# The second half of an MLP: 24 pairs of K tiles in sliding groups, all by seven products, their sums gathered in DRAM

## The chip, the cores and the metric

The kernel runs on one core of one Trainium2 chip. The metric is the device time of one execution in microseconds (us), as the median of several runs. TensorE is PE in the views of the profile, VectorE is DVE, ScalarE is ACT, GpSimd is POOL and SyncE is SP.

## The reference

One layer of a decoder on 512 rows of width 2048: a mixer of gated linear attention and mLSTM heads, a layer norm, an MLP with squared ReLU, and a second layer norm. The change lies in the second matrix product of the MLP.

```
def _sq_relu_mlp(u, w_ff1, w_ff2):
    return jnp.square(jax.nn.relu(u @ w_ff1)) @ w_ff2
...
    u = x * (1.0 + sc2) + sh2
    y = _sq_relu_mlp(u, w_ff1[l], w_ff2[l])
    x = _layer_norm(ALPHA * x + g2 * y, ln2_g[l], ln2_b[l])
```

`w_ff1` is 2048 x 8192 and `w_ff2` 8192 x 2048. The hidden matrix h (512 x 8192) is the left operand of the second product.

## The kernel before

**Split operands.** Every float32 operand of a matmul is split into a high and a low part: ACT casts the high part, DVE subtracts it to get the low part, and PE multiplies high by high, high by low and low by high into the same bank of PSUM. So each product costs three matmuls.

**First half of the MLP.** w_ff1 is worked through in 16 blocks of 512 columns, each over 8 steps (units) of two K tiles. From the third block on, a unit is a Strassen-like 2 x 2 scheme with seven products in place of eight: each product is 6 matmuls of 256 columns, and it has a PSUM bank of its own. `w_operands` prepares the weight side of such a unit: a cast of three quarters as they are (`bh`), four sums of quarters on DVE (`w_combos`), a cast of the sums (`th`, in the views `hi`), and two subtractions (`bl`, 768 wide, and `tl`, in the views `lo`, 1024 wide). A unit is prepared two units ahead (`LOOK`), and its tiles have three buffers. At the end of a block the seven banks are combined by two copies on ACT and seven additions on DVE; ReLU, square and a store of h to the DRAM tiles `hd` follow.

**Second half.** h comes back from `hd` in pairs of K tiles. 30 pairs go through 4 column blocks of 512; the last two pairs (`tail`) are added while the layer norm runs. The 30 pairs are cut into chunks of 8, 8, 8 and 6. For each chunk the four column blocks follow one another, and one pass over a chunk for one block (a sweep) keeps its sums in PSUM. A pair is of kind S (seven products, 42 matmuls of 256 columns) or C (eight products as plain matmuls, 24 of 512 columns). The four chunks have 4, 5, 4 and 0 pairs of kind S, over four blocks 52 S units and 44 + 24 C units.

`load` prepares the h side of a pair (`h_operands`): for S an own set of casts on ACT and of sums and subtractions on DVE, once for the four sweeps that use it; for C two casts and two subtractions. Loads of the next chunk are spread over the last sweep of the chunk before. At the end of a sweep one ACT copy and DVE additions empty the banks into `z` in SBUF (`evac1` to `evac3`).

**What sets the order.** DVE and ACT run their instructions exactly as the code issues them (`MANUAL`): in each pass of the unit loop first the operands of unit n + 2, then the jobs of unit n (loads among them), then the matmuls of unit n, then, after the last unit of a sweep, its emptying. PE, SP and POOL follow an order that the framework chooses. PSUM has eight banks, handed out in turn by `mm_bank`.

Of the kernel before, what the change touches and what calls it, by code (L numbers as in the profile page):

```python
# [16 lines left out]
P = 128  # L17
# [41 lines left out]
def trunk_layer_kernel(  # L59
# [989 lines left out]

    pa21 = tc.alloc_tile_pool(name="pa21", bufs=1, side="right")  # L1050
# [72 lines left out]
    def sums_add(i):  # L1123
# [30 lines left out]
    def w_combos(raw, name, f_slot):  # L1154
        b12, b11, b22, b21 = (raw[:, j * HB:(j + 1) * HB] for j in range(4))
        f = f_slot(name + "f")
        t3, n1, t2, t4 = (f[:, j * HB:(j + 1) * HB] for j in range(4))
        V.tensor_tensor(n1, b11, b12, ALU.subtract)  # L1158
        V.tensor_tensor(t3, b22, b12, ALU.subtract)  # L1159
        V.tensor_tensor(t2, b22, n1, ALU.add)  # L1160
        V.tensor_tensor(t4, b21, t2, ALU.subtract)  # L1161
        return f

# [6 lines left out]
    def w_ops(bh, bl, th, tl):  # L1170
        def op(h, l, j):
# [3 lines left out]
                7: op(th, tl, 0), 5: op(th, tl, 1), 6: op(th, tl, 2), 4: op(th, tl, 3)}  # L1175
# [49 lines left out]
    def assign(kinds):  # L1225
        free, out, odd = {"h": 16, "l": 16, "s": NS}, [], False
        for kind in kinds:
            want = ("hhhhlll", "hhhllll")[odd] if kind == "S" else "hhll"
            odd ^= kind == "S"
            if want.count("h") > free["h"] or want.count("l") > free["l"]:  # L1230
                n = len(want)
                want = ("s" * min(n, free["s"]) + "h" * free["h"] + "l" * free["l"])[:n]
            for g in want:
                free[g] -= 1
            assert min(free.values()) >= 0
            out.append(want)
        return out
# [109 lines left out]
    for nb in range(2, DFF // CB):  # L1347
        pb = {m: mm_bank(f"fp{nb}_{m}", (P, 2, HB)) for m in ORDER}
        for i in range(KP):
# [10 lines left out]
            if nb == DFF // CB - 1 and i in EARLY:  # L1360
                load(0, EARLY.index(i))
# [302 lines left out]
```

## Time and profile before

| | us |
|---|---|
| median of 3 runs | 2192.06 (2190.67 to 2193.08) |
| the profiled execution, its own time | 2191.13 |
| its span | 2189.1 |
| PE busy | 2134.7 (98%) |
| DVE busy | 1689.8 (77%) |
| ACT busy | 861.5 (39%) |
| POOL busy | 125.9 (6%) |

The span is the time from the first to the last recorded instruction; some 2 us of the execution's own time lie around it. Busy time is summed over records, and neighbouring records of one engine can overlap by some tens of nanoseconds, so the spacing of starts tells what an instruction costs in a row. The granted TensorE clock is 1.00 of its full level in every stretch shown below. In the part of the page on DMA queues there is no queue that POOL's software feeds: every transfer of data is issued from SP.

### The profile page before, as it was taken

Reading aid. Unit: us, or ns where it says so; the run is one execution under the profiler, and the core shown is the slowest. Engines: PE = TensorE matmul, PEld = TensorE weight load, DVE = VectorE, ACT = ScalarE, POOL = GpSimd, SP = SyncE. Lnnn points to the kernel's source line nnn. Section 1 sums busy time; section 2 is a strip of 40 time slices with the busy share of each in tenths; the row PEclk is TensorE's granted clock in tenths of the full one; section 3 lists DMA queues with packets and bytes.
Section 4 is the critical chain, followed back from the end, with each engine's and each line's share of the span. In section 5 each row is a group of like instructions: output and inputs, shape, how many; then the busy total and the mean of one; then the engine's idle time right before and its main releaser. Section 6 shows DMA issues by size and latency. Waiting matters only on the chain.

```text
span 2189.1 us, 33107 instructions
## 1 busy us (share of the span) xinstructions
PE 2134.7 (98%) x13105; PEld 1909.0 (87%) x13105; DVE 1689.8 (77%) x2848; ACT 861.5 (39%) x1184; POOL 125.9 (6%) x107
## 2 busy tenths in 40 slices
PE   6989999999999999999999999999999999999997
PEld 4767788888888888999999999999999999998886
DVE  7986677667776878888788788788768779666678
ACT  4222544243332135454454454455334334323223
POOL 3334200100000000000000000000000000000002
PEclk9999999999999999999999999999999999999999
DMA  8875345666678766444444444355334335335562
GB/s 312 273 271 177 119 136 154 215 217 226 216 236 303 273 207 225 141 130 151 128 132 136 126 136 135 116 163 174 106 106 154 119 105 164 125 103 186 169 199 85
DMA packets 174407, 374.81 MB, mean 171 GB/s; under 512 B 16032, under 2 KB 18300, under 8 KB 174252
## 3 DMA queue, kind: packets, MB, share of 16 engines
q1 hardware_dynamic: 174252, 372.70, 52.3%
q8 instruction: 102, 1.67, 0.3%
q14 instruction: 53, 0.43, 0.1%
HBM read 347.40 MB, written 25.18 MB: 170 GB/s over the span
## 4 chain that ended last, share of the span: by engine, by line
PE 82%; DVE 7%; DMA 6%; ACT 2%; issue 2%; POOL 0%; SPq 0%; DVEq 0%; ACTq 0%; POOLq 0%
PE fp L1357 9%; PE fp L1358 9%; PE fp L1356 9%; PE gp_c L1450 3%; PE gp_c L1451 3%; PE gp_c L1452 3%; DMA wr<-in_w_ada_dram 3%; DVE wr L162 2%; PE gp L1436 2%; PE gp L1438 2%; PE gp L1439 2%; PE gp L1545 2%; PE gp L1547 2%; PE gp L1546 2%; PE gp_c L1439 2%
## 5 line engine op out<-in xcount | busy, mean ns | idle before, releaser
L162 DVE SCALAR_TENSOR_TENSOR wr<-wr,csb 128x1024 f32<-128x1024 f32 x192 | 256.9, 1358 | 28.5 <-DMA wr<-in_w_ada_dram 28.2
L1598 POOL TENSOR_TENSOR l2lrs<-l2lrs,neghalf 128x1 f32<-128x1 f32 x3 | 1.6, 543 | 1307.7 <-DVE l2lrs L1597 1307.7
L1161 DVE TENSOR_TENSOR z<-f,z 128x256 f32<-128x256 f32 x125 | 53.1, 425 | 4.3
L1158 DVE TENSOR_TENSOR z<-f 128x256 f32<-128x256 f32 x125 | 52.4, 419 | 0.0
L1159 DVE TENSOR_TENSOR z<-f 128x256 f32<-128x256 f32 x125 | 52.4, 419 | 0.0
L1160 DVE TENSOR_TENSOR z<-f,z 128x256 f32<-128x256 f32 x125 | 52.4, 419 | 0.0
L1382 ACT ACTIVATE z<-z 128x1024 f32<-128x1024 f32 x28 | 28.1, 1052 | 54.7 <-DVE z L1377 54.7
L1189 DVE TENSOR_TENSOR f_0lo<-z,f_0hi 128x1024 fp32r<-128x1024 f32 x17 | 20.8, 1226 | 22.3 <-ACT f_0hi L1185 22.3
L1185 ACT CAST f_4hi<-z 128x1024 fp32r<-128x1024 f32 x17 | 17.9, 1053 | 43.5 <-DVE z L1161 43.5
L1185 ACT CAST f_0hi<-z 128x1024 fp32r<-128x1024 f32 x17 | 17.8, 1049 | 38.3 <-PE fp L1357 24.5
L1189 DVE TENSOR_TENSOR f_1lo<-z,f_1hi 128x1024 fp32r<-128x1024 f32 x14 | 17.2, 1226 | 18.5 <-ACT f_1hi L1185 18.5
L654 DVE TENSOR_TENSOR gqk<-gqk,st 128x512 f32<-128x512 f32 x40 | 25.3, 679 | 7.5 <-PE st L223 7.3
L654 DVE TENSOR_TENSOR gv<-gv,st 128x512 f32<-128x512 f32 x40 | 25.2, 679 | 5.9 <-PE st L230 5.8
L1189 DVE TENSOR_TENSOR f_7lo<-z,f_7hi 128x1024 fp32r<-128x1024 f32 x14 | 17.2, 1226 | 15.1 <-ACT f_7hi L1185 15.1
L126 DVE TENSOR_TENSOR ul<-uf,uh 128x512 fp32r<-128x512 f32 x16 | 11.9, 752 | 21.0 <-ACT uh L125 21.0
L1386 ACT ACTIVATE z<-z 128x1024 f32<-128x1024 f32 x28 | 28.0, 1048 | 0.0
L832 ACT ACTIVATE y<-mo,dd 128x256 f32<-128x256 f32 x16 | 7.6, 475 | 51.9 <-DVE dd L825 51.9
L1185 ACT CAST f_6hi<-z 128x1024 fp32r<-128x1024 f32 x14 | 14.7, 1053 | 29.6 <-DVE z L1161 29.6
L1185 ACT CAST f_1hi<-z 128x1024 fp32r<-128x1024 f32 x14 | 14.7, 1049 | 29.5 <-PE fp L1357 26.5
L1185 ACT CAST f_5hi<-z 128x1024 fp32r<-128x1024 f32 x14 | 14.7, 1051 | 28.9 <-DVE z L1161 28.9
L1185 ACT CAST f_7hi<-z 128x1024 fp32r<-128x1024 f32 x14 | 14.7, 1049 | 28.7 <-PE fp L1357 24.5
L1373 DVE TENSOR_TENSOR z<-z,fp 128x512 f32<-128x512 f32 x14 | 9.6, 688 | 20.7 <-PE fp L1358 20.7
(2266 smaller groups left out, 8781.9 us busy)
## 6 DMA issues: line engine op xcount, KB each, us to landing
f<-in_w_ff_dram SPq DMA_DIRECT2D x232, 512.0 KB, 3.8
wr<-in_w_ada_dram SPq DMA_DIRECT2D x192, 512.0 KB, 4.7
hd<-z SPq DMA_DIRECT2D x32, 512.0 KB, 3.9
hr<-hd SPq DMA_DIRECT2D x26, 512.0 KB, 3.5
z<-in_x_dram SPq DMA_DIRECT2D x4, 1024.0 KB, 5.4
xd<-z SPq DMA_DIRECT2D x4, 1024.0 KB, 8.5
x<-xd SPq DMA_DIRECT2D x16, 256.0 KB, 4.4
wl<-in_w_ff_dram SPq DMA_DIRECT2D x8, 512.0 KB, 4.7
```

The source lines that it names most:

```text
L162: V.scalar_tensor_tensor(raw, raw, 1.0, csb[:, h * DH:(h + 1) * DH], ALU.mult, ALU.mult, accum_out=msum[:, h, v * KT + k:v * KT + k + 1])
L1158: V.tensor_tensor(n1, b11, b12, ALU.subtract)
L1161: V.tensor_tensor(t4, b21, t2, ALU.subtract)
L1185: A.copy(th, f)
L1189: V.tensor_tensor(tl, f, th, ALU.subtract)
L1356: T.matmul(o, lhsT=wh[:, sl], rhs=q[:, 0], start=i == 0 and j == 0, stop=False)
L1357: T.matmul(o, lhsT=wh[:, sl], rhs=q[:, 1], start=False, stop=False)
L1358: T.matmul(o, lhsT=wl[:, sl], rhs=q[:, 0], start=False, stop=i == KP - 1 and j == 1)
L1439: T.matmul(o, lhsT=ql[:, sl], rhs=wh, start=False, stop=last and own and j == 1)
L1450: T.matmul(o[:, cl], lhsT=qh[:, sl], rhs=hi[:, t, cl], start=False, stop=False)
L1451: T.matmul(o, lhsT=qh[:, sl], rhs=lo[:, t], start=False, stop=False)
L1452: T.matmul(o, lhsT=ql[:, sl], rhs=hi[:, t], start=False, stop=last and t == 1)
```

## The change

All 24 pairs of the first three chunks become kind S (96 units); the six pairs of the last chunk stay C. The chunks give way to groups of two pairs. A round takes up to four neighbouring groups (8 units) through one column block, and the next round drops the oldest group, takes in a new one and goes on to the next block, so that each pair is used in four rounds in a row. There are 15 rounds of 2, 4, 6, 8 (nine times), 6, 4 and 2 units. Two pairs are loaded per full round, for the even pair at its first unit, for the odd one at its fifth.

Every round holds its seven sums in seven banks and ends with `evac`: ACT copies the banks two by two into a scratch of 128 x 1024 in `z` (three such pieces in turn), and each filled piece goes to the DRAM tile `sums` of its block. The first round of a block stores it from SP; the eleven later ones add it with an accumulating transfer, issued from POOL. In the plain sweeps at the end `sums_load` brings the sums back (28 transfers of 256 KB), and `z_sums` combines them on DVE (7 additions for each block). The signs of the scheme are turned so that two sums of 256 columns with a common term become one instruction of 512, in the weights of both halves and in h. The seven PSUM additions that empty a block of the first half stay seven.

```diff
@@ -1154,12 +1160,15 @@
     def w_combos(raw, name, f_slot):
         b12, b11, b22, b21 = (raw[:, j * HB:(j + 1) * HB] for j in range(4))
         f = f_slot(name + "f")
-        t3, n1, t2, t4 = (f[:, j * HB:(j + 1) * HB] for j in range(4))
-        V.tensor_tensor(n1, b11, b12, ALU.subtract)
-        V.tensor_tensor(t3, b22, b12, ALU.subtract)
+        n1, t3, t2, t4 = (f[:, j * HB:(j + 1) * HB] for j in range(4))
+        V.tensor_tensor(halves(f[:, :S]), halves(raw[:, HB:3 * HB]),
+                        b12.unsqueeze(1).to_broadcast([P, 2, HB]), ALU.add)
         V.tensor_tensor(t2, b22, n1, ALU.add)
-        V.tensor_tensor(t4, b21, t2, ALU.subtract)
+        V.tensor_tensor(t4, b21, t2, ALU.add)
...
-    NS = 17
-    CHUNKS = ["SCSCSCSC", "SCSSCSSC", "SCSCSCSC", "CCCCCC"]
-    SLOTS = [assign(kinds) for kinds in CHUNKS]
+    NS, SP, GP, CP = 28, 24, 2, 6
+    S_SLOTS = ("hhhhlll", "hhhllll", "hhhhlll", "hhhllll", "hhllsss") + ("sssssss",) * 3
...
-        a1 = slot(tags[2], f"hb{ft}")
-        split(a1[:, :HB], a1[:, HB:], raw[:, 0, :HB])
-        f = f_slot(f"hf{ft}")
-        s1, s2, s3, s4 = (f[:, j * HB:(j + 1) * HB] for j in range(4))
-        a11, a21, a12, a22 = (raw[:, t, o:o + HB] for t in range(2) for o in (0, HB))
-        V.tensor_tensor(s1, a21, a22, ALU.add)
+        a2h, a2l, a1, c1h, c1l, c2h, c2l = (slot(g, f"h{ft}_{i}") for i, g in enumerate(tags))
+        a11, a21, a12, _ = (raw[:, t, o:o + HB] for t in range(2) for o in (0, HB))
+        f = f1_slot(f"hf{ft}")
+        s3, s1, s2, s4 = (f[:, j * HB:(j + 1) * HB] for j in range(4))
+        A.copy(a2h, raw[:, 1])
+        A.copy(a1[:, :HB], a11)
+        V.tensor_tensor(halves(f[:, :S]), a21.unsqueeze(1).to_broadcast([P, 2, HB]),
+                        raw.rearrange("p t (o c) -> p (t o) c", o=2)[:, 0:4:3], ALU.subtract)
         V.tensor_tensor(s2, s1, a11, ALU.subtract)
-        V.tensor_tensor(s3, a11, a21, ALU.subtract)
-        V.tensor_tensor(s4, a12, s2, ALU.subtract)
-        s12 = h_split(f[:, :S], tags[3:5], f"hc{ft}")
-        s34 = h_split(f[:, S:], tags[5:7], f"hd{ft}")
+        V.tensor_tensor(s4, a12, s2, ALU.add)
+        A.copy(c1h, f[:, :S])
+        A.copy(c2h, f[:, S:])
+        V.tensor_tensor(a2l, raw[:, 1], a2h, ALU.subtract)
+        V.tensor_tensor(a1[:, HB:], a11, a1[:, :HB], ALU.subtract)
+        V.tensor_tensor(c1l, f[:, :S], c1h, ALU.subtract)
+        V.tensor_tensor(c2l, f[:, S:], c2h, ALU.subtract)
...
+    NG = SP // GP
+    units = []
+    for r in range(NG + 3):
+        ps = [GP * g + e for g in range(max(0, r - 3), min(NG - 1, r) + 1) for e in range(GP)]
+        units += [("S", (r + 1) % NCB, 2 * p, p == ps[0], p == ps[-1]) for p in ps]
+    NU = len(units)
+    for b in range(NCB):
+        units += [("C", b, 2 * (SP + i), i == 0, i == CP - 1) for i in range(CP)]
+    tail = 2 * (SP + CP)
...
+    for p in range(GP, SP + CP):
+        use = [u[2] for u in units].index(2 * p)
+        n = max(1, use - 6 + 3 * (p % 2)) if p < SP else NU - 10 + 2 * (p - SP)
+        at(n, lambda p=p: load(p))
+        if p >= 2 * GP:
+            at(n - 2, lambda p=p: fetch(2 * p, p % 2))
...
+    sums = [hdram.tile([P, 7 * S], F32, name=f"sums{b}") for b in range(NCB)]
+    begun = set()
+    def evac(pb, b):
+        for i in range(0, 7, 2):
+            ms = ORDER[i:i + 2]
+            st_ = scratch("st", 2, 3)[:, :len(ms) * S]
+            for e, m in enumerate(ms):
+                A.copy(halves(st_[:, e * S:(e + 1) * S]), pb[m])
+            o = sums[b][:, i * S:(i + len(ms)) * S]
+            if b in begun:
+                G.dma_start(o, st_, accum_op=ALU.add)
+            else:
+                nc.sync.dma_start(o, st_)
+        begun.add(b)
+    def sums_load(b, q):
+        for i, m in enumerate(ORDER):
+            q[m] = f3_slot(f"q{b}_{m}")
+            nc.sync.dma_start(q[m], sums[b][:, i * S:(i + 1) * S])
...
+        if last and kind == "S":
+            evac(pb, b)
```

Where ACT stands at the border of the two halves: after the last copy out of the first half's last block (`fp`) come, before, loads of pairs (`ha` to `hd`) and the operands of units 2 and 3 (`f_0_4`, `f_0_6`).

```order
L1371 COPY z<-fp_3_14003 128x2x256
L125 CAST ha_14510<-z 128x512
L125 CAST hb_14514<-z 128x256
L125 CAST hc_14521<-z 128x512
L125 CAST hd_14525<-z 128x512
L1181 CAST f_0_4bh<-f_0_4_14529 128x768
L1185 CAST f_0_4hi<-z 128x1024
L125 CAST ha_14585<-z 128x512
L125 CAST hb_14589<-z 128x512
L1382 ACTIVATE z<-z 128x1024 x2
L125 CAST f_0_6hi<-f_0_6_14595 128x1024
L125 CAST ha_14627<-z 128x512
```

Now the operands of units 2 and 3 (`f_2_0`, `f_2_2`), the ReLU and square of the last block and the load of pair 2 (`h_0` to `h_5`) stand in front of the first copy of the first round's banks (`gp_1`).

```order
L1376 COPY z<-fp_3_13897 128x2x256
L1190 CAST f_2_0bh<-f_2_0_14414 128x768
L1387 ACTIVATE z<-z 128x1024 x2
L1194 CAST f_2_0hi<-z 128x1024
L1391 ACTIVATE z<-z 128x1024 x2
L1273 CAST h_0_14475<-z 128x512
L1274 CAST h_2_14477<-z 128x256
L1279 CAST h_3_14478<-z 128x512
L1280 CAST h_5_14480<-z 128x512
L1190 CAST f_2_2bh<-f_2_2_14493 128x768
L1194 CAST f_2_2hi<-z 128x1024
L1457 COPY z<-gp_1_14407 128x512
```

The seven copies that empty the first round stand behind the operands of unit 3, though that round ends with unit 1.

Where ACT empties a full sweep, before (second chunk, block 1): one copy between the operands of the next block.

```order
L1185 CAST f_2_16hi<-f_2_16f 128x1024
L1465 COPY fq_1_0_16950<-gp_1_1_16591 128x2x256
L125 CAST f_2_18hi<-f_2_18_16957 128x1024
L1181 CAST f_2_20bh<-f_2_20_16999 128x768
L1185 CAST f_2_20hi<-f_2_20f 128x1024
L1181 CAST f_2_22bh<-f_2_22_17057 128x768
```

Now, after the fourth round (block 0; the next units are `f_1_4` to `f_1_8`):

```order
L1190 CAST f_1_6bh<-f_1_6_15632 128x768
L1194 CAST f_1_6hi<-z 128x1024
L1457 COPY z<-gp_1_15202 128x512
L1457 COPY z<-gp_2_15203 128x512
L1457 COPY z<-gp_3_15204 128x512
L1457 COPY z<-gp_7_15205 128x512
L1457 COPY z<-gp_5_15206 128x512
L1457 COPY z<-gp_6_15207 128x512
L1457 COPY z<-gp_4_15208 128x512
L1190 CAST f_1_8bh<-f_1_8_15705 128x768
L1194 CAST f_1_8hi<-z 128x1024
L1273 CAST h_0_15718<-z 128x512
```

Seven copies follow one another; the operands of the next round's third unit (`f_1_8`) and the load of a pair (`h_0`) stand behind them.

Where DVE prepares the weights of one S unit, before (`f_1_20`, block 1, K tiles 20 and 21):

```order
L1158 TENSOR_TENSOR f_1_20f<-f_1_20_16599 128x256
L1159 TENSOR_TENSOR f_1_20f<-f_1_20_16599 128x256
L1160 TENSOR_TENSOR f_1_20f<-f_1_20_16599,f_1_20f 128x256
L1161 TENSOR_TENSOR f_1_20f<-f_1_20_16599,f_1_20f 128x256
L1188 TENSOR_TENSOR f_1_20bl<-f_1_20_16599,f_1_20bh 128x768
L1189 TENSOR_TENSOR f_1_20lo<-f_1_20f,f_1_20hi 128x1024
```

And now:

```order
L1164 TENSOR_TENSOR z<-f_1_20_17560 128x512
L1166 TENSOR_TENSOR z<-f_1_20_17560,z 128x256
L1167 TENSOR_TENSOR z<-f_1_20_17560,z 128x256
L1197 TENSOR_TENSOR f_1_20bl<-f_1_20_17560,f_1_20bh 128x768
L1198 TENSOR_TENSOR f_1_20lo<-z,f_1_20hi 128x1024
```

Two sums have become one of twice the width, and each of the two sums left reads the result of the instruction ahead of it.

## Rows read from the trace of the kernel before

**Rows 1.** Busy time in three stretches of the second half: engines, clock, DMA.

```profile
core 0: us, PE busy (x) PEld busy (x) DVE busy (x) ACT busy (x) POOL busy (x), PEclk, DMA share, GB/s
1500.00:1540.00 40.00, 39.59 (x255) 35.83 (x254) 35.41 (x63) 23.10 (x33) 0.00 (x0) 1.00 0.45 148
1820.00:1860.00 40.00, 40.00 (x275) 37.20 (x274) 38.45 (x67) 19.03 (x29) 0.00 (x0) 1.00 0.53 170
2060.00:2100.00 40.00, 40.00 (x179) 33.12 (x178) 27.75 (x38) 9.71 (x11) 0.00 (x0) 1.00 0.55 165
```

**Rows 2.** Waits of PE from 1510 us to the end.

```profile
PE gp_c L1439 <- DVE hd L126: 0.2, 1, 0.2
PE gp L1436 <- ACT f_8hi L1185: 0.2, 1, 0.2
```

**Rows 3.** Timeline of PE: start us, us, engine, line, operation.

```profile
1499.87 0.28 PE L1436 MATMUL gp<-f_0bh,hb 128*128 128x256 f32 x1
...
1679.16 0.28 PE L1436 MATMUL gp<-f_20bh,hb 128*128 128x256 f32 x1
...
1684.17 0.28 PE L1436 MATMUL gp<-f_22bh,hb 128*128 128x256 f32 x1
...
2002.07 0.39 PE L1545 MATMUL gp<-f_48hi,hb 128*128 128x512 f32 x1
```

**Rows 4.** Timeline of DVE in the last columns of the first half.

```profile
1474.60 0.68 DVE L126 TENSOR_TENSOR ha<-hr,ha 128x512 fp32r<-128x512 f32 x1
...
1477.78 0.69 DVE L126 TENSOR_TENSOR hd<-z,hd 128x512 fp32r<-128x512 f32 x1
1478.38 0.42 DVE L1158 TENSOR_TENSOR z<-f 128x256 f32<-128x256 f32 x1
...
1479.05 0.42 DVE L1160 TENSOR_TENSOR z<-f,z 128x256 f32<-128x256 f32 x1
1479.51 0.42 DVE L1161 TENSOR_TENSOR z<-f,z 128x256 f32<-128x256 f32 x1
1479.85 0.95 DVE L1188 TENSOR_TENSOR f_5bl<-f,f_5bh 128x768 fp32r<-128x768 f32 x1
1481.13 1.22 DVE L1189 TENSOR_TENSOR f_5lo<-z,f_5hi 128x1024 fp32r<-128x1024 f32 x1 [0.32 <-ACT f_5hi L1185]
1482.27 0.69 DVE L126 TENSOR_TENSOR ha<-hr,ha 128x512 fp32r<-128x512 f32 x1
```

**Rows 5.** Timeline of DVE where a column block of the first half is emptied.

```profile
1459.14 0.69 DVE L1373 TENSOR_TENSOR z<-z,fp 128x512 f32<-128x512 f32 x1 [1.48 <-PE fp L1358]
1459.86 0.69 DVE L1374 TENSOR_TENSOR z<-z,fp 128x512 f32<-128x512 f32 x1
...
1462.98 0.42 DVE L1158 TENSOR_TENSOR z<-f 128x256 f32<-128x256 f32 x1
```

**Rows 6.** Timeline of ACT: casts, and a copy out of PSUM.

```profile
1477.65 0.83 ACT L1181 CAST f_5bh<-f 128x768 fp32r<-128x768 f32 x1
1480.04 1.05 ACT L1185 CAST f_5hi<-z 128x1024 fp32r<-128x1024 f32 x1 [1.56 <-DVE z L1161]
...
1538.16 1.06 ACT L1185 CAST f_0hi<-z 128x1024 fp32r<-128x1024 f32 x1 [2.26 <-DVE z L1161]
1539.12 0.58 ACT L1465 COPY fq<-gp 128x512 f32<-128x512 f32 x1
1539.59 1.06 ACT L125 CAST f_2hi<-f 128x1024 fp32r<-128x1024 f32 x1
```

**Rows 7.** DMA issues: out<-in, queue, count, KB each, median us to landing.

```profile
hd<-z SPq DMA_DIRECT2D x32, 512.0 KB, 3.9
hr<-hd SPq DMA_DIRECT2D x26, 512.0 KB, 3.5
...
xd<-z SPq DMA_DIRECT2D x4, 1024.0 KB, 8.5
...
out_dram<-z SPq DMA_DIRECT2D x16, 256.0 KB, 2.3
```

More of the change, by code (lines that the diff above doesn't have):

```diff
@@ L1432, in seven @@
             (wh, wl), (qh, ql) = ops[m], hq[m]
[L1433 removed]
             for j in range(2):
[L1435 to L1437 removed]
+                o, sl = pb[m][:, j], slice(j * P, (j + 1) * P)
+                T.matmul(o, lhsT=qh[:, sl], rhs=wh, start=first and j == 0, stop=False)
                 T.matmul(o, lhsT=qh[:, sl], rhs=wl, start=False, stop=False)
[L1439 removed]
+                T.matmul(o, lhsT=ql[:, sl], rhs=wh, start=False, stop=last and j == 1)
@@ L1441, in plain @@
     def plain(pb, ops, hq, first, last):
         hi, lo = ops
-        for t in range(2):
-            qh, ql = hq[t]
-            for tt in range(NT):
-                o, sl = pb["C"][tt], slice(tt * P, (tt + 1) * P)
-                for cl in ((slice(0, HB), slice(HB, CB)) if first and t == 0 and tt > 1
-                           else (slice(0, CB),)):
-                    T.matmul(o[:, cl], lhsT=qh[:, sl], rhs=hi[:, t, cl], start=False, stop=False)
-                T.matmul(o, lhsT=qh[:, sl], rhs=lo[:, t], start=False, stop=False)
-                T.matmul(o, lhsT=ql[:, sl], rhs=hi[:, t], start=False, stop=last and t == 1)
@@ new lines, in plain @@
+        for tt in range(NT):
+            sl = slice(tt * P, (tt + 1) * P)
+            for t in range(2):
+                uh, ul = hq[t]
+                T.matmul(pb[tt], lhsT=uh[:, sl], rhs=hi[:, t], start=first and t == 0, stop=False)
+                T.matmul(pb[tt], lhsT=uh[:, sl], rhs=lo[:, t], start=False, stop=False)
+                T.matmul(pb[tt], lhsT=ul[:, sl], rhs=hi[:, t], start=False, stop=last and t == 1)
+    sums = [hdram.tile([P, 7 * S], F32, name=f"sums{b}") for b in range(NCB)]
@@ new lines, in z_sums @@
+    def z_sums(b, q):
+        c11, c12, c21, c22 = (z[:, b, 2 * i:2 * i + 2, o:o + HB] for i in range(2) for o in (HB, 0))
+        p = {m: halves(t) for m, t in q.items()}
+        V.tensor_tensor(c11, p[1], p[2], ALU.add)
+        V.tensor_tensor(p[6], p[1], p[6], ALU.add)
+        V.tensor_tensor(p[7], p[6], p[7], ALU.subtract)
+        V.tensor_tensor(p[6], p[6], p[5], ALU.subtract)
+        yield
+        V.tensor_tensor(c12, p[3], p[6], ALU.subtract)
+        V.tensor_tensor(c21, p[7], p[4], ALU.add)
+        V.tensor_tensor(c22, p[5], p[7], ALU.subtract)
+        yield
@@ new lines, in trunk_layer_kernel @@
+    g2b = []
+    for n, (kind, b, ft, first, last) in enumerate(units):
+        if first and kind == "S":
+            pb = {m: mm_bank(f"gp{n}_{m}", (P, 2, HB)) for m in ORDER}
+        elif first:
+            pb = [mm_bank(f"gp{n}_{t}") for t in range(NT)]
+            if b == 0:
+                for i in range(NCB):
+                    g2b.append(f3_slot(f"g2b{i}"))
+                    nc.sync.dma_start(g2b[i], rowd[G2][0:1, blk(i)].broadcast_to([P, CB]))
+            if b < 2:
+                for i in range(2):
+                    q = {}
+                    at(n + 3 * i, lambda q=q, i=2 * b + i: sums_load(i, q))
+                    steps = z_sums(2 * b + i, q)
+                    for j in range(2):
+                        at(n + 3 * i + 1 + j, lambda steps=steps: next(steps))
+            x2, gb = [], []
+            at(n, lambda b=b, gb=gb: gb.append(ln_rows(ln1_g, ln1_b, b, f"ln1r{b}")))
+            for t in range(NT):
+                at(n + 1 + t, lambda b=b, x2=x2, t=t: last_load(b, x2, t))
+                at(n + 2 + t, lambda x2=x2, gb=gb, t=t: last_x2(x2, gb[0], t))
+            if b == 0:
+                for i in range(2):
+                    at(n + 3 + 2 * i, lambda i=i: tail_h(i))
+            if b == 2:
+                for i in range(2):
+                    at(n + 1 + 2 * i, lambda i=i: tail_w(0, i))
+            if b == 3:
+                for i in range(2, 7):
+                    at(n - 1 + min(i, 5), lambda i=i: tail_w(i // 2, i % 2))
```

169 lines of the change are left out of this document (29 added, 140 removed).

## The prediction

> **What bounds the kernel now.** The busy times by stretch come first. In the second half PE is busy for 40.00 of 40 us at a granted clock of 1.00, while DVE lies between 27.75 (plain sweeps) and 38.45 us, and only the stretch at the border of the two halves has 39.59 [rows 1]. The list of PE's waits agrees: 0.4 us from 1510 us to the end [rows 2]. So PE sets the time, with DVE close behind. The timeline of PE then gives the stage: from its first matmul at 1499.87 to that of the plain sweeps at 2002.07 are 502.2 us, and an S unit takes 1684.17 - 1679.16 = 5.01 us [rows 3]. The timelines of DVE and ACT say what an instruction costs in a row of others, by the distance of starts [rows 4 to 6], and the list of DMA issues what a transfer takes [rows 7].
>
> **What PE saves.** The stage has 52 S and 44 C units now, and 96 S units afterwards: 96 x 5.01 = 481.0 us, 21.2 less, if PE never waits. The six plain pairs and the tail stay.
>
> **What DVE has to do for it.** On DVE, 512 columns cost 0.60 in a row (1477.78 to 1478.38) and 0.72 where the next instruction reads the result (1459.14 to 1459.86); 256 columns cost 0.34 (1479.51 to 1479.85) and 0.46 (1479.05 to 1479.51) [rows 4, 5].
> - One S unit takes 1482.27 - 1478.38 = 3.89 [rows 4]. Its four sums cost 1.47 of that; the new three cost 0.72 + 0.46 + 0.34 = 1.52, since each is followed by its reader. So a unit costs 3.94: merging the sums gains nothing. In the first half that is hidden under 5.01 of PE.
> - One load of an S pair took 1478.38 - 1474.60 = 3.78 [rows 4], and takes 0.72 + 0.46 + 0.34 + 0.60 + 0.34 + 0.60 + 0.60 = 3.66.
> - A full round is 8 units and 2 loads: 31.52 + 7.32 = 38.84 on DVE against 8 x 5.01 = 40.08 on PE. DVE may lose 1.24 us in a round, no more.
>
> **What the emptying of a round costs.** ACT runs in the order written, so the seven copies stand behind the cast of the sums of unit n + 2, and the casts of the following unit stand behind the copies. PE needs the first copy for the second product of the next round, as seven of eight banks are in use. A copy of 512 columns from PSUM starts 0.96 after the cast ahead of it, lasts 0.58, and the next starts 0.47 later [rows 6]. Count from the first copy's start, a. Two copies are done at a + 1.05 and their transfer starts; the seventh copy writes into the same scratch, so it waits until a transfer of length L has landed: a + 1.1 + L. The cast `bh` of the next unit starts 0.48 after that and ends 0.83 later [rows 6], at a + 2.4 + L, when DVE can go on with `bl`. Without that wait DVE would have done `tl` and the three sums and stood there at a + 2.8. It stands still for L - 0.35, gets 0.3 back because the cast of the sums is then ready, and so loses L - 0.67. Queued behind the waiting copy on ACT are two casts and the four of a load; DVE waits for these, PE for DVE, and the next round's copies for DVE's sums. The loop closes: a full round lasts 38.84 + L - 0.67 = 38.2 + L, or 40.08 if that is longer. Every us of L above 1.9 is paid in every round.
>
> **L.** Rounds 3 and 4 still end in plain stores of 512 KB from SBUF to DRAM, as `hd<-z`, 3.9 us [rows 7]: 2 x 2.0 = 4.0 us. The seven full rounds after them wait for accumulating transfers, of which the trace has none. The lowest bound is the shortest store, 256 KB in 2.3; the upper one the store of 1024 KB in 8.5, as an accumulation moves 512 KB from SBUF and reads 512 KB of DRAM [rows 7]. Store and read of 512 KB one after the other would be 3.9 + 3.5 = 7.4, side by side 3.9 [rows 7]. I take the middle, 5.5: 7 x 3.6 = 25.2 us; by the bounds 2.8 and 46.2. A gain below nothing is excluded, as the copies are new on this path.
>
> The Trainium skill has a price for L: DMA: Bandwidth & Descriptors, "Anatomy of one DMA — SWDGE (gpsimd) path", fits 2.0 us plus the bytes over 436 GB/s, and Collectives: The Full Stack, "The bandwidth ceiling: the fold count and why AG ≠ RS ≠ AR", says that an adding transfer is slower because it reads two sources through one ring, not because of the add. Together they estimate 2.0 + 2 x 1.2 = 4.4 us, by which the rounds would cost 17.5 us in place of 25.2 and the forecast would be 2206. No row of this trace shows such a transfer; the plain store of 3.9 [rows 7] already takes longer than the 3.2 of that fit.
>
> **The border.** DVE and ACT reach the second half without a lead, because two loads (at 1474.60 the first begins [rows 4]) come before it and four follow in its first nine units. Take the chain up to the third round's emptying, the one behind unit 11: 6 loads x 3.66 = 22.0, operands of 16 units x 3.94 = 63.0 (three of the first half, 0 to 12 of the second), seven additions for the first half's last block 3.84 + 0.60 = 4.4 [rows 4, 5], to the copy's start in unit 13's operands 2.7, and two earlier emptyings at 3.9 - 0.35, less 0.3 for one, some 7: first copy at about 1474.6 + 99.1 = 1573.7, done at 1574.3. On PE alone, unit 12 would ask for that bank at 1499.87 + 12 x 5.01 + 0.72 = 1560.7. So 13.6 us are lost there, some 6 at each of the first two rounds: the first round ends with unit 1, near 1510, but its first copy stands behind the operands of unit 3, near 1516. Between 8 (PE's order brings one product of the next unit ahead of the wait, which saves up to 0.7 each time) and 17.
>
> **What costs nothing.** In the plain sweeps DVE has 12 of 40 us free [rows 1]; the 28 additions of `z_sums`, 28 x 0.6 to 0.72, some 18 us over 66, fit in. The 28 reads of 256 KB go in front of weights that are asked for two units (11 us) ahead; without that cover some 3 us. The last three rounds have few loads, and DVE's slack there covers the emptying.
>
> **Sum.** -21.2 + 13.6 + 4.0 + 25.2 = +21.6. The profiled execution took 2191.13, so 2212.7; the median of the runs lies 0.9 above it, so I predict 2214. By the bounds of L, 2191 and 2235; with those of the border, 2186 to 2239.
>
> **Rivals.**
> - The copies hide (faster). If DVE is quicker than its rows say, or ACT reaches the copies while PE still fills the last bank, the chain per round stays under 40.08 and PE alone counts: -21.2 + some 3 at the border, 2174. It decides from L under 1.9, or from DVE's round under 36.5 with L at 4. For it: PE lost only 0.4 us in a stretch where DVE was busy 35.41, and nothing where it was busy 38.45 [rows 1]. Against it: there nothing on ACT waited for a transfer, and no store row is under 2.3 [rows 7]. Chance 0.13.
> - The waits eat the gain. L near 2.3 to 3: -21.2 + 13.6 + 4.0 + 7 x 0.4 to 1.1 = 2191 to 2196. Chance 0.13.
> - Accumulation is much slower than any store, since a new path through POOL issues it: L of 12 gives 7 x 10.1 = 71 and 2260. No row speaks against it but that 1024 KB take 8.5 [rows 7]. Chance 0.12.
> - The forecast, L from 3 to 9, has 0.62; its own range is 2196 to 2238.
>
> For 8 in 10 I give 2187 to 2240. A measurement of this kernel tells 0.2% (4.4 us) from no change; by that faster has 0.13, within 0.2% 0.13, slower 0.74.
>
> **What would show it.** Right: PE waits at the second product of each round, for a copy on ACT (`gp_2`), some 5 us at the first two rounds and 3.6 at the full ones; ACT stands before the seventh copy of a round and its releaser is the transfer to `sums`; DVE stands before `bl` of the next round's third unit, and its releaser is `bh` on ACT; full rounds are 38.2 + L apart; S units stay at 5.01; no wait in the plain sweeps. Wrong: PE busy 40 of 40 through the full rounds, or transfers that land within 2 us. If PE waits, but for `bl` or `tl` in the middle of rounds, DVE's own sum was the larger.

## The result: 50 us slower, and the profile after

The changed kernel takes 2241.36 us (median of 4 runs, 2236.1 to 2247.92), the kernel before in the same comparison 2191.36: a ratio of 1.0231, 95% interval 1.0201 to 1.026. Forecast were 2214 and a range up to 2240, so the sign was right, and the time lies just above the range. The profiled execution took 2247.92 us, with a span of 2246.2, which is 57.1 longer than before. It is the longest of the four runs, so the stages below add up to a little more than the medians differ.

The busy times by stretch, of the kernel after (columns as in [rows 1]):

```profile
1500.00:1540.00 40.00, 33.94 (x261) 32.64 (x259) 33.50 (x54) 24.19 (x37) 0.00 (x0) 0.96 0.52 178
1820.00:1860.00 40.00, 35.69 (x293) 34.88 (x292) 30.69 (x48) 19.30 (x29) 3.40 (x4) 1.00 0.64 163
2020.00:2060.00 40.00, 33.62 (x216) 30.20 (x215) 18.56 (x25) 18.66 (x30) 6.38 (x9) 0.96 1.05 288
2060.00:2100.00 40.00, 37.33 (x161) 30.13 (x162) 29.57 (x41) 10.20 (x13) 0.83 (x1) 1.00 0.63 193
```

PE was busy for 40 of 40 us in the full sweeps [rows 1]. In a full round it now has 35.69, and DVE has less work per us, not more: both wait. In the third row the share of the DMA engines is 1.05, with no engine of the core but PE busy for half of the stretch.

PE's waits from 1510 us to the end (engine, matmul line, what was waited for: us in total, times, longest); before there were 0.4 us [rows 2]:

```profile
PE gp L1434 <- ACT z L1457: 13.1, 10, 3.8
PE gp L1435 <- DVE f_2bl L1197: 5.2, 2, 2.8
PE gp L1435 <- DVE f_14bl L1197: 3.4, 2, 2.0
```

Two of these waits, in the order of time, at the second product of the eighth round (`f_16` and `f_18` are its first two units):

```profile
1750.89 0.39 PE L1435 MATMUL gp<-f_18bl,h 128*128 128x256 f32 x1 [1.32 <-DVE f_18bl L1197]
1751.66 0.39 PE L1434 MATMUL gp<-f_16bh,h 128*128 128x256 f32 x1 [0.38 <-ACT z L1457]
```

ACT's waits up to the last emptying (at 2059 us), and DVE's within the full rounds; of DVE's, one such line stands for each accumulating round:

```profile
ACT z L1457 <- DMA sums<-z: 61.5, 15, 6.8
...
DVE f_24bl L1197 <- ACT f_24bh L1190: 7.0, 1, 7.0
```

One round shows the chain: timelines of ACT, of POOL and of DVE at the end of the seventh round.

```profile
1751.03 3.02 ACT L1457 COPY z<-gp 128x512 f32<-128x512 f32 x6
1759.24 0.59 ACT L1457 COPY z<-gp 128x512 f32<-128x512 f32 x1 [5.19 <-DMA sums<-z]
1759.72 0.84 ACT L1190 CAST f_20bh<-f 128x768 fp32r<-128x768 f32 x1
```

```profile
1752.45 2.79 POOL L1460 DMA_DIRECT2D sums<-z  x3 [36.63 <-ACT z L1457]
1760.19 0.86 POOL L1460 DMA_DIRECT2D sums<-z  x1 [4.94 <-ACT z L1457]
```

```profile
1760.59 0.96 DVE L1197 TENSOR_TENSOR f_20bl<-f,f_20bh 128x768 fp32r<-128x768 f32 x1 [6.69 <-ACT f_20bh L1190]
```

Six copies run together from 1751.03. The first piece's transfer is issued at 1752.45. The seventh copy, which writes into the same piece, starts at 1759.24. DVE stands for 6.69 us before `bl` of the third unit of the next round, since its `bh` stands behind that copy.

The issues of the transfers of sums (columns as in [rows 7]):

```profile
sums<-z POOLq DMA_DIRECT2D x33, 512.0 KB, 8.5
q<-sums SPq DMA_DIRECT2D x28, 256.0 KB, 5.8
sums<-z SPq DMA_DIRECT2D x12, 512.0 KB, 4.8
sums<-z POOLq DMA_DIRECT2D x11, 256.0 KB, 7.3
```

An accumulating transfer of 512 KB lands after 8.5 us, a plain one of the same size after 4.8 (medians).

The bounds of the stage on PE, to be held against 1499.87 and 2002.07 [rows 3], are these:

```profile
1500.09 0.28 PE L1434 MATMUL gp<-f_0bh,h 128*128 128x256 f32 x1
...
2046.30 0.41 PE L1444 MATMUL gp<-f_48hi,hb 128*128 128x512 f32 x1
...
2187.96 0.39 PE L1547 MATMUL fl<-wl,hb 128*128 128x512 f32 x1
```

The 96 S units take 546.2 us in place of 502.2. The plain sweeps, up to the first matmul of the tail (`fl`), take 141.7 us; before they took 130.6 (`fl` began at 2132.63). What follows takes 58.2 in place of 56.5. Within the stage the first copies of the rounds stand at 1575.05 (third round), 1617.74, 1660.14, then 45.3 apart up to 1976.95 (the last full round). With 5.01 us for a unit this gives:

| part | predicted | measured |
|---|---|---|
| PE saves | -21.2 | -21.2 (481.0 of matmuls) |
| border, first three rounds | +13.6 | +14.8 (what remains of 546.2) |
| two full rounds with plain stores | +4.0 | +4.9 (85.1 against 80.2) |
| seven full rounds that accumulate | +25.2 | +36.3 (316.8 against 280.6) |
| rounds of 6, 4 and 2 units | 0 | +9.2 (69.3 against 60.1) |
| plain sweeps | 0 | +11.1 |
| tail, and ahead of the stage | 0 | +2.0 |
| sum | +21.6 | +57.1 |

### The profile page after: what moved, and what is told of

The parts are those of the page before. It is cut to its first block, busy times and chain, and to the rows that moved or that the text cites. A ratio compares the mean times of both kernels' runs of the same rounds, so it can differ in the third digit from the quotient of the medians.

```text
span 2246.2 us, 34969 instructions
## 1 busy us (share of the span) xinstructions
PE 2140.0 (95%) x13873; PEld 1942.7 (86%) x13873; DVE 1757.1 (78%) x2802; ACT 950.3 (42%) x1343; POOL 163.1 (7%) x151
## 4 chain that ended last, share of the span: by engine, by line
PE 56%; issue 18%; DVE 13%; DMA 8%; ACT 3%; POOL 1%; SPq 0%; ACTq 0%; POOLq 0%; DVEq 0%
PE fp L1362 8%; PE fp L1361 8%; PE fp L1363 8%; DMA wr<-in_w_ada_dram 3%; DVE wr L162 3%; DMA sums<-z 1%; PE wo_0b L228 1%; PE wo_0b L230 1%; PE wo_0b L229 1%; PE gp L1445 1%; PE gp L1444 1%; PE gp L1446 1%; DMA f<-in_w_ff_dram 1%; POOL sums L1460 1%; DVE z L1164 1%
## 5 line engine op out<-in xcount | busy, mean ns | idle before, releaser
L1164 DVE TENSOR_TENSOR z<-f 128x512 f32<-128x512 f32 x208 | 142.4, 685 | 0.0
L1460 POOL DMA_DIRECT2D sums<-z x44 | 37.9, 866 | 1175.3 <-DVE f_10lo L1198 813.9
L1166 DVE TENSOR_TENSOR z<-f,z 128x256 f32<-128x256 f32 x208 | 88.4, 425 | 7.2
L1167 DVE TENSOR_TENSOR z<-f,z 128x256 f32<-128x256 f32 x208 | 88.4, 425 | 7.2
L1457 ACT COPY z<-gp 128x512 f32<-128x512 f32 x105 | 54.2, 601 | 72.7 <-DMA sums<-z 61.5
L654 DVE TENSOR_TENSOR gv<-gv,st 128x512 f32<-128x512 f32 x40 | 25.2, 679 | 6.2 <-PE st L230 6.2
L1198 DVE TENSOR_TENSOR f_2lo<-z,f_2hi 128x1024 fp32r<-128x1024 f32 x18 | 22.1, 1226 | 5.8 <-ACT f_2hi L1194 5.8
L1198 DVE TENSOR_TENSOR f_6lo<-z,f_6hi 128x1024 fp32r<-128x1024 f32 x18 | 22.1, 1225 | 5.8 <-ACT f_6hi L1194 5.8
```

The costliest lines, as they stand in the source:

```text
L654: V.tensor_tensor(o, o, src, ALU.add)
L1164: V.tensor_tensor(halves(f[:, :S]), halves(raw[:, HB:3 * HB]), b12.unsqueeze(1).to_broadcast([P, 2, HB]), ALU.add)
L1167: V.tensor_tensor(t4, b21, t2, ALU.add)
L1198: V.tensor_tensor(tl, f, th, ALU.subtract)
L1457: A.copy(halves(st_[:, e * S:(e + 1) * S]), pb[m])
L1460: G.dma_start(o, st_, accum_op=ALU.add)
```

## The experiments

The part ahead of the stage varies from execution to execution: the first matmul of the second half lies between 1488.2 and 1500.1 us in these traces, and PE's busy time in the first 200 us, which no experiment touches, between 161.7 and 170.0. So stages are compared by their length, and kernels by the medians. Each kernel has one trace; the ratios are worked out from all its executions and can differ a little from the quotient of two medians.

**Seven slots.** The seventh copy gets a tile of its own, so that it waits for no transfer of its own round.

```diff
...
-            st_ = scratch("st", 2, 3)[:, :len(ms) * S]
+            st_ = (scratch("st", 2, 3) if i < 6 else
+                   ff3.tile([P, S], F32, tag="st7", bufs=1, name=f"st7_{len(turn7)}"))
...
```

> The seventh copy of a round gets a scratch of 128 x 512 of its own, so that it waits for no transfer of its own round; all else stays. Theory A (the wait of ACT for the accumulating transfer closes a loop ACT, DVE, PE): without it DVE is held only about 1.1 us per round (seven copies at 0.5 and the cast, less what DVE has left to do), so full rounds last 40.1 us in place of 45.3, the transfers still take some 8 us, and the kernel takes about 2185 (2178 to 2195). Theory B (the traffic of the accumulation, or POOL's writing of descriptors, slows DVE, PE or the weights' loads): full rounds stay above 43 us and the kernel above 2220.

Measured: 2185.4 us against 2188.81 of before, ratio 0.9995 (0.9979 to 1.0011). ACT's copies at the ends of two neighbouring full rounds, then DVE's wait before `bl` of a round's third unit (7.0 in the changed kernel), then the busy times at the border, in a full round and at the start of the plain sweeps:

```profile
1798.11 3.02 ACT L1459 COPY z<-gp 128x512 f32<-128x512 f32 x6
1800.97 0.65 ACT L1459 COPY st<-gp 128x512 f32<-128x512 f32 x1
1838.13 3.02 ACT L1459 COPY z<-gp 128x512 f32<-128x512 f32 x6
```

```profile
DVE f_24bl L1197 <- ACT f_24bh L1190: 1.4, 1, 1.4
```

```profile
1490.00:1530.00 40.00, 33.02 (x255) 32.22 (x256) 36.31 (x59) 24.58 (x38) 0.00 (x0) 0.95 0.57 191
1820.00:1860.00 40.00, 40.00 (x339) 40.00 (x338) 35.62 (x56) 21.73 (x31) 3.50 (x4) 1.00 0.68 178
1980.00:2000.00 20.00, 15.49 (x69) 12.49 (x67) 2.43 (x3) 3.83 (x7) 2.40 (x3) 1.00 1.06 287
2000.00:2020.00 20.00, 18.62 (x70) 14.80 (x71) 16.16 (x23) 6.21 (x7) 0.00 (x0) 0.83 0.50 158
```

The rounds are 40.0 us apart and PE is busy in all of it, though the transfers are no faster (8.7 us for 512 KB). The stage takes 490.1 us in place of 546.2: the wait of one copy cost 56 us. Of the 65.2 us that the stage lost in four lines of the table, 9.1 are left: some 9 at the border and 0.8 in the last three rounds (60.9 for 12 units), less 0.8 that the full rounds stay below 8 x 5.01. The kernel is then level with the one before: the stage is 12.1 us shorter than its 502.2, but the plain sweeps are 10.5 longer (141.0) and what follows them 5.1 (61.6).

**Plain stores.** Every piece is stored plainly from SP, in place of being added; the addition is left out.

```diff
-                G.dma_start(o, st_, accum_op=ALU.add)
+                nc.sync.dma_start(o, st_)
```

> The eleven accumulating transfers become plain stores from SP of the same size to the same place (the sums of earlier rounds are overwritten, so the addition is left out). Theory A: the loop stays and only L changes, from about 8 to 4.8 us; full rounds go from 45.3 to 42.5 us, as the two full rounds after plain stores have now, and the kernel takes about 2211 (2203 to 2219). Theory C (it is the copies on ACT by themselves that cost, the transfer is beside the point): no change, 2236 to 2246.

Measured: 2214.67 us, ratio 1.013 (1.0094 to 1.0166). Copies at the end of a round, and the stores:

```profile
1741.71 3.02 ACT L1457 COPY z<-gp 128x512 f32<-128x512 f32 x6
1747.30 0.59 ACT L1457 COPY z<-gp 128x512 f32<-128x512 f32 x1 [2.58 <-DMA sums<-z]
1784.33 2.04 ACT L1457 COPY z<-gp 128x512 f32<-128x512 f32 x4
```

```profile
sums<-z SPq DMA_DIRECT2D x45, 512.0 KB, 4.6
```

The wait is still there and is shorter, 2.58 in place of 5.19; the rounds are some 42.6 apart (one is 43.95). The plain sweeps (from 2019.99 to 2151.50) take 131.5 us, as before the change, although the same 28 reads of sums stand in SP's queue. So what the sweeps lose is tied to the accumulating transfers: without them the reads cost 0.9 us.

**A larger ring for POOL's transfers.**

```diff
-                   dynamic_dma_scratch_size=2048)
+                   dynamic_dma_scratch_size=4096)
```

> The scratch for the descriptors of POOL's transfers is doubled from 2048 to 4096 bytes per partition. Theory A1 (the transfer takes its 8 us for moving and adding): landing stays at 8.0 to 8.5 us and the kernel at 2236 to 2248. Theory D (POOL waits for room in that scratch): landing drops below 6.5 us, full rounds below 44, kernel near 2225.

Measured: 2239.68 us, ratio 1.0247 (1.022 to 1.0274); a transfer of 512 KB lands after 9.2 us, no sooner than before, and the rounds stay 45.2 apart. Theory D is out: twice the room for POOL's descriptors does not make them faster.

**Subtractions on POOL.** Two of the seven DVE instructions of each S load move to POOL.

```diff
-        V.tensor_tensor(c1l, f[:, :S], c1h, ALU.subtract)
-        V.tensor_tensor(c2l, f[:, S:], c2h, ALU.subtract)
+        G.tensor_tensor(c1l, f[:, :S], c1h, ALU.subtract)
+        G.tensor_tensor(c2l, f[:, S:], c2h, ALU.subtract)
```

> Two of the four subtractions of each load of an S pair (512 columns each) move from DVE to POOL; the wait for the transfer stays. Theory A (a full round lasts DVE's sum plus the hold): DVE's sum falls by 4 x 0.6 = 2.4 us per full round and by some 7 us at the border, so full rounds go to about 42.9 and the kernel to about 2213 (2207 to 2222). Theory E (DVE and POOL get in each other's way, or POOL's subtractions come late behind the transfers on its queue): DVE's subtractions become longer than 0.69 us or its waits move to the loads, full rounds stay above 44.5, kernel 2230 or more.

Measured: 2263.06 us, ratio 1.0363 (1.0336 to 1.039), 22 us slower than the changed kernel. POOL and DVE side by side in one load:

```profile
1767.70 1.29 POOL L1283 TENSOR_TENSOR h<-z,h 128x512 fp32r<-128x512 f32 x1 [3.12 <-PE gp L1436]
1768.95 1.73 POOL L1284 TENSOR_TENSOR h<-z,h 128x512 fp32r<-128x512 f32 x1
```

```profile
1767.74 1.79 DVE L1281 TENSOR_TENSOR h<-z,h 128x512 fp32r<-128x512 f32 x1
1769.46 1.50 DVE L1282 TENSOR_TENSOR h<-z,h 128x256 fp32r<-128x256 f32 x1
```

In the changed kernel, where POOL computes nothing in these rounds, the same two (columns: times, us in total, mean ns):

```profile
L1281 DVE TENSOR_TENSOR h<-z,h 128x512 fp32r<-128x512 f32 x16 | 10.9, 684 | 0.0
L1282 DVE TENSOR_TENSOR h<-z,h 128x256 fp32r<-128x256 f32 x16 | 6.7, 419 | 0.0
```

DVE's two remaining subtractions take 1.79 and 1.50 us here, and 1.35 and 1.51 in the mean of 15 loads, in place of 0.68 and 0.42. What DVE hands over (two at 0.60) it pays again by longer instructions, and the rounds grow to some 47.5. The Trainium skill has the rule: SBUF — State Buffer, "Who interferes with whom", says that a DVE instruction with two SBUF inputs contends with a GpSimd instruction that reads SBUF. The trace agrees.

**The border and the plain sweeps of the kernel with seven slots.** Six more kernels build on the first experiment. Two questions were open: why the border still loses 9 us, and why the plain sweeps take 141.0.

The first brings the last unit of a round, and its emptying, ahead of the operands and loads of the same pass:

```diff
+        early = last and kind == "S"
+        if early:
+            seven(pb, ahead.pop(0), hops[ft], first, last)
+            evac(pb, b)
         prepare2(n + LOOK)
...
```

> As the kernel with the seventh scratch, and after the last unit of a round the matmuls and the seven copies stand ahead of the operands of unit n + 2 and of the loads. Theory A (at the border the copies come late because they stand behind operands and loads that DVE has not reached): the wait of about 6 us behind the first round goes, and what stays is DVE's own sum at the border, some 5 us, seen as waits for bl; about 4 us faster than with the seventh scratch alone, 2181. Theory F (ACT, held at the copies until PE has done the unit, now brings the next round's operands late): waits for bh and bl in every full round, 2190 or more.

Measured: 2194.0 us, ratio 1.0035 (1.0016 to 1.0054). The border gained 1.0 us (from the first matmul to the third round's first copy 68.3 in place of 69.3), and the stage is 489.6. That does not clear the copies' place on ACT, because one wait took the place of another. The 6.5 us that PE waited there for `bl` and `bh` of `f_2` are gone, and 5.7 us of waits for copies have come; the first copies now stand for a store of h out of the same scratch:

```profile
1510.40 3.03 ACT L1459 COPY z<-gp 128x512 f32<-128x512 f32 x6 [3.02 <-DMA hd<-z]
```

What the border costs beyond the waits for `sums` stays open. The time lies in theory F's range, but not by its mechanism, as the full rounds stay 40.0 apart: the plain sweeps became longer, 148.8 us. Why this order lengthens them stays open too.

The next two change the reads of sums on top of that: once from POOL's queue, once one block per plain sweep.

```diff
-            nc.sync.dma_start(q[m], sums[b][:, i * S:(i + 1) * S])
+            G.dma_start(q[m], sums[b][:, i * S:(i + 1) * S])
```

> As the one before, and the 28 reads of the sums are issued from POOL instead of SP. Theory G (in the plain sweeps the weights' loads stand behind the reads of the sums on SP's queue): the waits for weights in the first two plain sweeps (7 to 10 us) go, 2173. Theory H (the DMA engines themselves are full there, whatever the queue): the wait stays, 2179 to 2183.

```diff
-            if b < 2:
-                for i in range(2):
-                    q = {}
-                    at(n + 3 * i, lambda q=q, i=2 * b + i: sums_load(i, q))
-                    steps = z_sums(2 * b + i, q)
-                    for j in range(2):
-                        at(n + 3 * i + 1 + j, lambda steps=steps: next(steps))
+            q = {}
+            at(n, lambda q=q, b=b: sums_load(b, q))
+            steps = z_sums(b, q)
+            for j in range(2):
+                at(n + 3 + j, lambda steps=steps: next(steps))
```

> As the kernel with the seventh scratch and the copies first, and the sums of one block are read in each of the four plain sweeps, in place of two in each of the first two; SP issues them. Both theories G and H expect shorter waits, since fewer reads fall together; H expects all of the gain here (2173) and none from the other queue, G expects less here than there (2176).

Measured: 2192.46 us, ratio 1.003 (1.0013 to 1.0046), and 2193.1 us, ratio 1.0028 (1.0011 to 1.0045). Their plain sweeps take 143.6 and 141.7 us: 5 and 7 less than with the changed order alone, but no less than with seven slots alone. Neither regains the 10 us, and no theory's time came. The spread reads without the changed order, as a control beside the experiment that follows:

> Seven slots as in the first experiment, and each plain sweep reads and combines the sums of its own block alone, with the two steps at its fourth and fifth unit, in place of two blocks in each of the first two sweeps. It is the control for the kernel with late plain stores. Theory J: the engines are full at the start of the plain sweeps by accumulating transfers, not by these reads, so the time stays at that of the seven slots alone, 2184 to 2188. Rival K: seven reads fewer ahead of the weights at the first sweep let it start on time, the plain sweeps fall to some 135 us and the time to 2179.

Measured: 2187.78 us, ratio 1.0006 (0.9991 to 1.0021); the plain sweeps take 138.5, 2.5 less than with seven slots alone, and what follows them 66.6 in place of 61.6, so the time stays, as theory J has it. Where the reads stand is thus at most a small part of the loss.

What then fills the DMA engines? The queues of the kernel with seven slots in the 40 us around the start of the plain sweeps (packets, MB, the time of the packets as a share of 16 engines; ahead of them the busy tenths of each us):

```profile
DMA  9999999999999999999999999999999999999999
...
q1 hardware_dynamic: 4560, 8.49, 58.3%
q0 software_dynamic: 1203, 3.75, 47.5%
```

No us is free. POOL's transfers, `q0`, take 47.5% of the engines' time for 3.75 MB, 12.7% for each MB; the plain ones take 6.9%. So it may be the accumulating transfers of the rounds of 6, 4 and 2 units, which come faster than those of full rounds, that keep the engines full just when the plain weights must come. The test is to store these last sums plainly into DRAM tiles of their own, and to let each plain sweep read and add them, with its own block's sums (`own` is true from the first unit of those rounds on):

```diff
+    late = {b: hdram.tile([P, 7 * S], F32, name=f"late{b}") for b in (1, 2, 3)}
...
-            o = sums[b][:, i * S:(i + len(ms)) * S]
-            if b in begun:
+            o = (late if own else sums)[b][:, i * S:(i + len(ms)) * S]
+            if b in begun and not own:
...
-            evac(pb, b)
+            evac(pb, b, n >= 84)
...
```

> Seven slots as in the first experiment, and the last three rounds (6, 4 and 2 units) store their sums plainly, from SyncE, into DRAM tiles of their own instead of adding them by accumulating transfers; each plain sweep then reads the sums of its own block, and those late ones (21 reads of 256 KB more), and DVE adds the two (21 additions of 512 columns, about 14 us, more). Nothing is left out. Theory J: the plain sweeps lose their 11 us because the accumulating transfers of the last rounds keep the DMA engines full (share 1.05 to 1.07) just when the weights of the plain sweeps are to come; with plain stores and late reads the sweeps take 131 to 135 us as with plain stores throughout (131.5), and the time is 2174 to 2179. Rival K: what is late are the weights because of their place in SyncE's queue, behind reads and stores that wait; 21 reads and 12 stores more in that queue make it no better, the sweeps stay at 141 us or more and the time at 2185 or above.

Measured: 2202.62 us, ratio 1.008 (1.0057 to 1.0103): slower. Its busy times in the first 80 us of the plain sweeps:

```profile
1980.00:2000.00 20.00, 20.00 (x97) 16.87 (x97) 6.69 (x8) 7.99 (x12) 0.00 (x0) 1.00 0.67 244
2000.00:2020.00 20.00, 20.00 (x90) 16.56 (x89) 17.31 (x25) 4.79 (x6) 0.00 (x0) 1.00 0.48 142
2020.00:2040.00 20.00, 20.00 (x90) 16.57 (x89) 6.47 (x9) 3.16 (x3) 0.00 (x0) 1.00 0.85 297
2040.00:2060.00 20.00, 14.87 (x49) 11.27 (x48) 17.91 (x27) 2.11 (x2) 0.00 (x0) 0.78 0.66 216
```

The first sweep is whole, PE busy for 20 of 20 us where seven slots had 15.49 and 18.62. The kernel with spread reads is the control: up to the end of the first sweep it differs from this one in the late stores alone. Its plain sweeps begin at 1987.93, and it loses time there (busy times, then a wait of PE):

```profile
1980.00:2000.00 20.00, 19.98 (x121) 17.61 (x120) 5.66 (x7) 7.94 (x13) 4.01 (x5) 1.00 1.07 256
2000.00:2020.00 20.00, 15.78 (x62) 12.37 (x62) 9.70 (x13) 4.64 (x6) 0.00 (x0) 0.91 0.63 187
PE gp L1444 <- ACT f_54hi L125: 3.5, 1, 3.5
```

With the accumulating transfers gone, the first sweep's loss is gone. But the third and the fourth sweep start late, by these waits of PE:

```profile
PE gp L1444 <- ACT f_48hi L125: 6.2, 1, 6.2
PE gp L1445 <- DVE f_48lo L126: 2.8, 1, 2.8
```

DVE has 11 additions in one piece ahead of their weights (for the third sweep from 2045.65 to 2052.52), after it stood some 4 us for rows of x from DRAM; all four sweeps take 150.4 us. Theory J's time did not come. The same with the reads and additions in portions of two or three:

```diff
-            at(n, lambda q=q, b=b: sums_load(b, q))
-            if b:
-                at(n + 1, lambda ql=ql, b=b: late_load(b, ql))
+            for j, ms in enumerate(((1, 2, 6), (7, 5), (3, 4))):
+                at(n + j, lambda q=q, ql=ql, b=b, ms=ms: sums_load(b, q, ql, ms))
+                at(n + (2, 3, 5)[j], lambda q=q, ql=ql, ms=ms: late_add(q, ql, ms))
...
```

> The kernel with late plain stores again (seven slots; rounds of 6, 4 and 2 units stored plainly apart), with the reads and additions of each plain sweep in small portions: reads of 3, 2 and 2 products at its first three units, late additions of 3, 2 and 2 at its third, fourth and sixth, and the two steps of combining at its fifth and sixth; at most 5 additions (3.5 us) stand in one unit of DVE, where 11 stood before. Nothing is left out. Theory J2: late stores freed the DMA engines for the first sweep (PE was busy 20 of 20 us from 1980 to 2020), and what made them slower in all were 11 additions and 14 reads in one piece ahead of the weights of the second and third sweep (PE busy 14.87 and 13.80 of 20 us); in portions the sweeps take 131 to 136 us and the time is 2176 to 2180, below the kernel before. Rival K2: what counts is how much is read, not in what portions (5.5 MB of late sums more); the sweeps stay at 143 us or more and the time at 2186 to 2200.

Measured: 2190.92 us, ratio 1.0018 (1.0004 to 1.0033); the sweeps take 138.1.

```profile
2040.00:2060.00 20.00, 20.00 (x90) 16.55 (x89) 19.62 (x29) 2.33 (x3) 0.00 (x0) 1.00 0.85 275
2060.00:2080.00 20.00, 20.00 (x90) 16.58 (x89) 16.79 (x25) 5.06 (x7) 0.00 (x0) 1.00 0.78 252
2080.00:2100.00 20.00, 16.76 (x66) 12.85 (x65) 17.12 (x25) 4.75 (x5) 0.00 (x0) 0.92 0.76 271
```

Now PE runs through to 2080, and loses 3.2 of 20 us after that, and 4.1 at the first matmuls of the tail. The theory is right on the first sweep, and the rival on the time; the sweeps' 138.1 lies between the two. What is saved early is lost late, and no run separates the 5.5 MB read again from the 21 additions. The lengths of the four plain sweeps, and of what follows them, in us:

| kernel | first | second | third | fourth | after them |
|---|---|---|---|---|---|
| before | 32.6 | 32.6 | 32.6 | 32.6 | 56.5 |
| changed | 37.5 | 38.9 | 32.6 | 32.6 | 58.2 |
| plain stores throughout | 32.7 | 33.6 | 32.6 | 32.6 | 60.4 |
| seven slots | 41.7 | 34.1 | 32.6 | 32.6 | 61.6 |
| seven slots, spread reads | 39.1 | 32.7 | 32.6 | 34.1 | 66.6 |
| late plain stores | 32.7 | 36.8 | 44.9 | 36.1 | 67.0 |
| late plain stores in portions | 32.7 | 32.6 | 33.2 | 39.6 | 65.8 |

By the control, 6.4 us of the first sweep (39.1 against 32.7) belong to the accumulating transfers. Every kernel that reads the sums block by block in all four sweeps has a longer end, 66 to 67 us; why is not shown. No version here beats the kernel before; the one with seven slots is level with it.

## Why the prediction was right in its chain and wrong in its size

**What PE saves: right.** An S unit stays at 5.01 us; in the full rounds of the experiment with seven slots, 8 units take 40.0.

**DVE's round of 38.84: it fits, as said.** With the wait gone, DVE is busy for 35.62 of 40 us and waits 1.4 us before `bl` once a round, and PE waits for nothing in the full rounds.

**The emptying of a round: right from the transfer to DVE, wrong in the last link.** The chain was to be: seventh copy, `bh` of the third unit, `bl` on DVE, PE. ACT's 61.5 us of waits for `sums` and DVE's 7.0 before `bl` stand where they were put. PE's waits do not. They were to stand before the second product, for a copy: 3.6 us in a full round, 5 at each of the first two. At the first two there is none; PE waits there 8.3 us for `bh` and `bl` of `f_2`. From the first full round on, the wait for a copy is 0.3 to 0.4 us five times and 1.2 to 3.8 in the last five rounds; PE's other waits in the full rounds are for `bl`, up to 2.0 us at a round's fourth unit. The prediction would have read those as a sign that DVE's own sum was the larger. That sign misled: with seven slots DVE does the same work, and they are gone. They were DVE's standstill, handed on to later units.

The formula was 38.2 + L for a round. Plain stores land in 4.6 to 4.8 and give 42.6, by the formula L = 4.4; the accumulating rounds give 45.3, so L = 7.1. In the timeline above the seventh copy starts 7.2 us after the second is done (1751.03 + 1.05 to 1759.24). L counts the first of a round's four transfers alone, which was issued at 1752.45; 8.5 us is the median over all of 512 KB. That the wait was the cause, and not DVE's sum, was only argued; the seven slots show it.

**L: the step that failed first.** It was taken as 5.5, the middle between a shortest store and a longest, and is 7.1. One row-based sum named in the prediction was close: a store and a read of 512 KB one after the other, 3.9 + 3.5 = 7.4 [rows 7]. Instead of that sum a middle was chosen, and 1.6 us in seven rounds make 11.1 us of the miss. That such a transfer does store and read in turn is not shown; only the number fits. The estimate of 4.4 us that the prediction worked out from the Trainium skill (DMA: Bandwidth & Descriptors, "Anatomy of one DMA — SWDGE (gpsimd) path", with two sources) lies further off; the measured 7.1 decides.

**The border: right in size,** 14.8 for 13.6. Of it, the waits of the first two emptyings were put at some 7; the seven slots took away 5.7 (from 75.0 to 69.3 between the first matmul and the third round's first copy). That leaves some 9, where the prediction had some 7 for DVE's backlog of operands and loads, so two terms missed by 1 to 3 us each and in part made up for each other: the near hit is in part luck. Whether those 9 are that backlog stays open, as said of the changed order.

**"What costs nothing": the step that failed second, and the larger,** 20.3 us against 11.1. It said that the last three rounds have few loads, so that DVE's slack covers the emptying. They lost 9.2 us, and 0.8 with seven slots. The slack of DVE is no cover, because DVE itself stands behind ACT's waiting copy, in a round of 2 units as in one of 8. The same step put the plain sweeps at nothing by DVE's free time, and at 3 us by the place of the reads in the queue. They lost 11.1, 4.8 in the first and 6.3 in the second. The trace of before shows the DMA share in the stretches used at 0.45 to 0.55 [rows 1], and the prediction did not add up the bytes where short rounds follow one another. There the share is 1.05. With late plain stores the first sweep's loss is gone; in the second, the runs do not separate the accumulating transfers from the reads, which alone cost 0.9.

**The rivals.** The copies hide: no, and with seven slots one sees what it would give, 2185, not the 2174 put down for it, as the border and the plain sweeps were priced at 3 and 0, and what follows the sweeps grew too. The waits eat the gain: no, L was not near 3. Accumulation much slower than any store: no, 8.5 is what the store of 1024 KB took [rows 7]. The forecast's mechanism held, with L inside its 3 to 9; its upper bound of 2239 was missed by the costs set to zero.

## What to carry over

When an engine that runs in order must wait for a transfer, price the transfer by a sum of the rows that it seems to be made of (here a store and a read in turn came within 0.3 us, though no run shows that it works so) rather than by the middle of two bounds, and count the wait in every round that has it, short rounds too: they have the same wait on less work. One more buffer at that place was worth 56 us here, and nothing else on the path had to become faster. A saving that turns on-chip sums into memory traffic must also be priced where rounds are shortest, by the share of the DMA engines there.

## What the runs showed of the hardware

- An accumulating transfer of 512 KB into DRAM lands after 8.5 to 9.7 us (medians of ten kernels), a plain store of the same size in the same kernels after 4.6 to 4.8. Around the start of the plain sweeps each accumulated MB takes 1.8 times the engines' time of the other traffic (12.7 against 6.9% of 40 us, seven slots). Doubling the ring did not shorten the landing.
- POOL's issue of such a transfer takes 0.86 us of its own time.
- Beside POOL's subtractions, DVE's subtractions of 512 and 256 columns take 1.35 and 1.51 us in the mean, in place of 0.68 and 0.42.
- PE stood for 5.43 us (seven slots, up to 2000.92), and its granted clock was then 0.50, the lower of its two levels, from 2002 to 2006, and 1.00 again from 2008. Matmuls of 512 columns start 0.43 us apart at that clock and 0.23 at 1.00. An estimate from these rows: the twelve matmuls from 2000.92 to 2007.02 took 6.1 us in place of 2.8, of which 0.46 was a further wait, so the stall cost some 3 us on top of its own length. In the changed kernel a shorter standstill was followed by the same: after the waits of 1.32 and 0.38 us shown with the result, the clock was 0.51 from 1753 to 1756.

```profile
2000.92 0.80 PE L1444 MATMUL gp<-f_54hi,hb 128*128 128x512 f32 x1 [5.43 <-ACT f_54hi L125]
2002.77 0.63 PE L1446 MATMUL gp<-f_54hi,hb 128*128 128x512 f32 x1
```
